# The prices of a list scheduler's calls, changed for three kinds of instruction, in a two-layer RWKV-7 trunk

## The chip, the cores and the metric

The kernel runs on one core of a Trainium2 chip. The metric is device time in microseconds: from the first to the last instruction of the program, plus what little lies around it. Three runs of the kernel before took 3034.83, 3038.67 and 3040.36 us, median 3038.67. One execution was profiled apart from these. Engines are named as in the profile: PE (TensorE matmuls), PEld (its weight loads), DVE (VectorE), ACT (ScalarE), POOL (GpSimd) and SP (SyncE, which only issues DMAs here).

## What is computed

One step of a hybrid decoder: a prompt of 16 + 512 rows and 8 sample rows go together through two layers of width 1024. All tensors are fp32. Each layer is

```
x = x + 0.5 * SwiGLU_1(RMSNorm(x))                          # d_ff 2816
x = x + W_o( sig(gA) * RWKV7(.) + sig(gB) * ShortConv(.) )  # the mixer
x = x + 0.5 * SwiGLU_2(RMSNorm(x))
```

with a last RMSNorm at the end. The recurrent part of the mixer, for 16 heads with a 64 x 64 state S each, is

```
Sa = S a_t
S  = S * w_t + Sa b_t^T + v_t k_t^T
y_t = S r_t
```

once from a zero state over the 528 prompt rows, and once for one step of 8 sample rows from given states.

## The kernel before

**Layout.** The 536 columns (528 prompt, 8 sample) lie along the free dimension, features along the 128 partitions. A fp32 product is made of three fp32r products: each operand is split into a high part (`hi`, a rounded copy by ACT) and a low part (`lo`, the rest, a subtraction on DVE), and `hi*hi + hi*lo + lo*hi` is summed. Weights arrive by DMA as `raw` and are split on the way.

**Stages.** The program alternates FFN stages (FFN 1 of layer 0; then the mixer; then FFN 2 of layer 0 and FFN 1 of layer 1; the mixer; FFN 2 of layer 1 and the last norm) with two mixer stages. An FFN stage is a stream of large fp32r matmuls.

**The mixer.** Heads are handled in eight pairs, p = 0 to 7. The 528 rows are cut into 11 chunks of 48. For each pair:

- `stage_k(p)`: projects k and r, forms decays, and by fp32 matmuls (`wg`) the triangular matrices of all chunks, `GT`. They go to DRAM (`td<-GT`) and come back in another layout (`Ta<-td`, `Tb<-td`). There the matrix I - T of all 22 chunk and head combinations is inverted by forward substitution on GpSimd: 47 steps of two dependent operations each, a product `pr<-Ta,Xinv` (later `pr<-Tb,Xinv`) and a sum `Xinv<-Xinv,pr`. There is one buffer each of `Ta`, `Tb` and `Xinv`. The inverse goes out by four DMAs `xd<-Xinv` and back by two, `Yd<-xd`; then `Xinv<-in_xid` loads the identity for the next pair.
- `stage_v(p)`: projects v and prepares per-chunk products (`wv`, `wg`, `wp`).
- `chain(p)`: the serial recurrence over the 11 chunks. Each chunk has five links through PE, all in tile `cq`: `cq<-mv,sd` (not in the first chunk), DVE `rh`, a transpose `cq<-cst,rh`, DVE `rd`, the product with the inverse `cq<-rd,Yd`, ACT `ud`, `cq<-GR,ud`, DVE `sx`, a transpose `cq<-cst,sx`, DVE `sd`. The last `sd` goes out as `out_o_swkv<-sd`.
- `gnorm(p)` normalises the chain's output (`wm` matmuls), `stage_m(p)` merges it with gates.

Beside these runs filler: 40 pieces of gates and short convolution (`gated_parts`, matmuls `acc<-xh,hi` and the like), handed out by a list per layer. After the last pair's projections `sample()` takes the 8 sample rows through one recurrent step: transposes, a trip through DRAM (`vd`, `VB`), then eight rounds of 512-column operations over the states `s`, mostly on GpSimd (`t` and `s` tiles; 88 such operations on GpSimd in the two layers together), another trip (`yd`, `yb`) and short norms. The tile `s` uses the buffer of `Ta`. The first half of the output projection w_o (`acc<-mh,hi` and the like, 192 matmuls) needs the sample's result and is the last filler of a mixer; the second half opens the next FFN stage.

**What sets the order.** Nothing is issued as it is written. Each call (`nc.vector.tensor_tensor(...)`) is put on a list by `Sched.add`, with a price from `Sched.price` (the time that the engine is thought to be busy) and its dependencies. At the end of a stage `flush` runs a list scheduling over five engines: it keeps a clock for each engine, takes the engine that is free first, and from the calls whose inputs and buffers are ready by its clock takes the one with the lowest priority number (`o.prio`: the place in the program less a `boost` for its kind of work). Time between engines is a table (`HOPS`). A result is ready for a dependent call on the same engine 0.1 to 0.15 us later. DMAs have a price on SP and a landing time. The order that comes out is fixed: each engine then executes its own queue in that order and waits at semaphores.

Prices of matmuls also go into `clocked`, which models PE's clock by the columns issued in steps of 3.4133 us. `self.ffn` is true within the body of an FFN; the change touches what is priced with it false, and the column count.

Of the kernel before, what the change touches and what calls it, by code (L numbers as in the profile page):

```python
# [8 lines left out]
F32R = mybir.dt.float32r  # L9
# [3 lines left out]
PSUM = bass.MemoryType.PSUM  # L13
# [83 lines left out]
class Sched:  # L97
# [41 lines left out]
    def price(self, eng, fn, out, ins, kw):  # L139
        n = self.width(out)  # L140
        if fn == "dma_start":
            return 0.48, 4 * n * out.shape[0] / self.DMA_RATE
        if eng == "tensor":
            if fn == "transpose" or kw.get("is_transpose"):
                return n / 1200 + 2e-3, self.HOP
            return (max(n, 256) / 2400 + (12e-3 if self.ffn else 2.3e-3) if ins[0].dtype == F32R else n / 600 + 6e-3), self.HOP
        if eng == "vector":
            if fn == "memset":
                return 8e-3 + n / 960, self.HOP
            if fn == "reciprocal":  # L150
                return 0.12 + n * 6.16e-3, self.HOP
            if fn == "tensor_reduce":
                n = self.width(ins[0])
            return (0.13 if len(ins) > 2 else 0.07) + n / 960, self.HOP
        if eng == "scalar":
            psum = any(x.tensor.space == PSUM for x in ins + [out])
            return (0.05 if psum else 0.095) + (0.09 if "scale" in kw else 0) + n / 1200, self.HOP
        if self.ffn:
            return 0.1 + n * 3.1e-3, self.HOP
        last = any(tuple(x.ap[-1])[0] == 0 for x in ins)  # L160
        return 0.155 + n * (1.63e-3 if last else 2.07e-3), self.HOP

    def add(self, eng, fn, args, kw):
        o = Op()
        o.seq, o.eng, o.fn, o.args, o.kw = len(self.ops), eng, fn, args, kw
        out = kw["out"] if "out" in kw else args[0]
        ins = [x for x in list(args) + list(kw.values()) if hasattr(x, "tensor") and x is not out]
        o.cost, o.lat = self.price(eng, fn, out, ins, kw)
        o.tab = TABLES.get(kw.get("func")) if eng == "scalar" else None
        o.succ, o.ready, o.prio, o.first, o.tiles, o.npred = [], 0.0, o.seq - self.boost, [], [], 0  # L170
        if eng == "tensor":
            o.cols0 = (o.cost - 2.3e-3) * 2400
            o.cols = o.cols0 * ins[0].shape[0] / 128
        w = (kw["lhsT"] if "lhsT" in kw else args[1]) if eng == "tensor" else None
        preds, needs, opens = {}, {}, {}
        for ap, wr in [(x, False) for x in ins] + [(out, True)]:
            t = ap.tensor
            if not hasattr(t, "tag_meta"):
                continue
            n = t.name  # L180
            if n not in self.acc:
                self.acc[n] = [], []
                if t.space != DRAM:
                    key = str(t.cap_key)
                    if key not in self.slots:
                        self.slots[key] = Slots(key.rsplit('_', 2)[1], t.bufs or t.tag_meta.bufs, self.gate)
                    self.life[n] = Life(self.slots[key], o)
                    self.slots[key].line.append(n)
                    o.first.append(n)
            if n not in o.tiles:  # L190
                o.tiles.append(n)
                if n in self.life:
                    lf = self.life[n]
                    lf.left += 1
                    opens[id(lf.opener)] = lf.opener
                    if n in lf.slots.held:
                        lf.slots.held[n] = None
            b = self.box(ap)
            writes, reads = self.acc[n]
            for c, q in writes + reads if wr else writes:  # L200
                if c[0] < b[1] and b[0] < c[1] and c[2] < b[3] and b[2] < c[3]:
                    preds[id(q)] = q
                    if not wr:
                        needs[id(q)] = 3 if ap is w and w.dtype == F32 else 2
            if wr:
                for a in (writes, reads):
                    a[:] = [x for x in a if not (b[0] <= x[0][0] and x[0][1] <= b[1] and b[2] <= x[0][2] and x[0][3] <= b[3])]
                writes.append((b, o))
            else:
                reads.append((b, o))  # L210

        for q in {**opens, **preds}.values():
            if q is o:
                continue
            kind = needs.get(id(q), 1 if id(q) in preds else 0)
            if q.succ is None:
                self.follow(q, o, kind)
            else:
                q.succ.append((o, kind))
                o.npred += 1  # L220
        self.ops.append(o)
# [1359 lines left out]
```

## Time and profile before

| | us |
|---|---|
| median of three runs | 3038.67 |
| profiled execution, its own time | 3028.59 |
| profiled execution, span | 3026.8 |
| mixer 1, from the end of the first FFN stage to the next | 395 to 1122 |
| mixer 2 | 1895 to 2626 |
| mean granted PE clock | 0.973 of full speed |

All five engines work side by side, so busy times overlap; matmul ends are modelled, so the starts of matmuls are the better measure. In the profile a fp32 matmul shows as two rows and a transpose as one. Buffer numbers are left out of names, so `mv0` and `mv1` are both `mv`. The views used: the head of the page, busy time by stretch of the span, waits by engine, groups by shape, and the timeline of one engine.

### The profile page before, as it was taken

To read this page: it belongs to the slowest core of one execution; us is meant where nothing else is said; L and a number is where in the kernel's file an instruction comes from. 1 tells how busy PE (TensorE), PEld (TensorE's weight loads), DVE (VectorE), ACT (ScalarE), POOL (GpSimd) and SP (SyncE) were. 2 spreads that over 40 slices of the span, in tenths; PEclk is the share of its full clock that TensorE was granted. 3 is DMA by queue.
4 is the path that set the end of the run, shared out by engine and by line. 5 is a ranking of instruction groups with operands and counts; after the bars stand their busy time and mean duration, and the time that the engine had idled before them with its cause. 6 is when DMAs were issued, how large, how long until landed. Compare 5 with 4: busy or idle time off the path is not lost. (4 is left out here: it accounts for less than half of the span.)

```text
span 3026.8 us, 56336 instructions
## 1 busy us (share of the span) xinstructions
PE 2835.8 (94%) x22146; PEld 2782.0 (92%) x22146; DVE 2170.7 (72%) x3995; ACT 1337.4 (44%) x2190; POOL 1043.2 (34%) x1886
## 2 busy tenths in 40 slices
PE   8999998988997899999999999999898988899997
PEld 8999998988897889999999999888888888899997
DVE  8777676766775868776687776766777659687774
ACT  5444453433443345444444444534444332554444
POOL 1000037776777811000100001477877778100001
PEclk9999999999999999999999999999999999999999
DMA  4233333223323462333323323332233133623232
GB/s 134 90 102 98 116 97 83 69 84 89 94 63 91 149 199 91 96 97 102 108 77 92 102 89 126 89 82 72 82 97 94 46 113 130 209 88 98 95 105 78
DMA packets 203802, 303.88 MB, mean 100 GB/s; under 512 B 102704, under 2 KB 110256, under 8 KB 203536
## 3 DMA queue, kind: packets, MB, share of 16 engines
q1 hardware_dynamic: 203536, 300.27, 32.7%
q8 instruction: 174, 2.85, 0.4%
q14 instruction: 92, 0.75, 0.1%
HBM read 264.49 MB, written 35.72 MB: 99 GB/s over the span
## 5 line engine op out<-in xcount | busy, mean ns | idle before, releaser
L268 ACT ACTIVATE hi<-raw 128x1024 fp32r<-128x1024 f32 (+4 forms) x460 | 387.4, 845 | 498.3 <-PE acc L268 188.9
L268 DVE TENSOR_TENSOR lo<-raw,hi 128x1024 fp32r<-128x1024 f32 (+4 forms) x460 | 461.0, 1004 | 78.6 <-ACT hi L268 71.8
L268 PE MATMUL acc<-xh,lo 128*128 128x268 f32 (+1 forms) x2112 | 484.5, 303 | 15.6 <-DVE lo L268 15.4
L268 PE MATMUL acc<-xh,hi 128*128 128x268 f32 (+1 forms) x2112 | 484.9, 304 | 11.4 <-ACT hi L268 4.8
L268 PE MATMUL acc<-xl,hi 128*128 128x268 f32 (+1 forms) x2112 | 482.3, 301 | 0.0
L268 POOL MEMSET wide<- 128x104 f32 (+1 forms) x7 | 1.3, 188 | 1328.7 <-DVE lo L268 1264.1
L268 POOL TENSOR_TENSOR Xinv<-Xinv,pr 88x140 f32<-88x140 f32 (+36 forms) x752 | 402.0, 535 | 54.8
L268 PEld LDWEIGHTS acc<-xh,lo 128*128 128x128 f32 x2112 | 350.2, 195 | 19.7 <-DVE lo L268 19.4
L268 PEld LDWEIGHTS acc<-xh,hi 128*128 128x128 f32 x2112 | 350.8, 195 | 16.8 <-ACT hi L268 8.3
L268 PEld LDWEIGHTS acc<-xl,hi 128*128 128x128 f32 x2112 | 348.4, 195 | 0.2
L268 PE MATMUL a<-hh,lo 128*128 128x268 f32 (+1 forms) x1408 | 287.6, 286 | 0.2 <-DVE lo L268 0.2
L268 PE MATMUL a<-hl,hi 128*128 128x268 f32 (+1 forms) x1408 | 287.2, 285 | 0.0
L268 PE MATMUL a<-hh,hi 128*128 128x268 f32 (+1 forms) x1408 | 286.5, 285 | 0.0
L268 POOL TENSOR_TENSOR pr<-Ta,Xinv 88x150 f32<-88x150 f32 (+21 forms) x384 | 200.0, 521 | 147.9 <-DMA Xinv<-in_xid 57.5
L268 PE MATMUL x<-xh,hi 128*128 128x268 f32 (+1 forms) x864 | 247.1, 286 | 1.6 <-ACT sn L268 1.6
L268 PE MATMUL x<-xl,hi 128*128 128x268 f32 (+1 forms) x864 | 247.0, 286 | 0.0
L268 PE MATMUL x<-xh,lo 128*128 128x268 f32 (+1 forms) x864 | 246.8, 286 | 0.0
L268 ACT ACTIVATE hi<-s 128x1024 fp32r<-128x1024 f32 x144 | 151.3, 1057 | 177.1 <-DVE s L268 101.3
L268 PEld LDWEIGHTS a<-hh,lo 128*128 128x128 f32 x1408 | 219.3, 188 | 0.5 <-DVE lo L268 0.4
L268 PEld LDWEIGHTS a<-hl,hi 128*128 128x128 f32 x1408 | 218.6, 188 | 0.0
L268 PEld LDWEIGHTS a<-hh,hi 128*128 128x128 f32 x1408 | 218.5, 188 | 0.0
L268 DVE TENSOR_TENSOR lo<-s,hi 128x1024 fp32r<-128x1024 f32 x144 | 173.4, 1221 | 16.5 <-ACT hi L268 15.7
(562 smaller groups left out, 7235.2 us busy)
## 6 DMA issues: line engine op xcount, KB each, us to landing
raw<-in_f_in SPq DMA_DIRECT2D x176, 512.0 KB
raw<-in_w_in SPq DMA_DIRECT2D x132, 512.0 KB
raw<-in_f_out SPq DMA_DIRECT2D x128, 256.0 KB
raw<-in_f_out SPq DMA_DIRECT2D x32, 384.0 KB
raw<-in_w_o SPq DMA_DIRECT2D x32, 256.0 KB
Ta<-td SPq DMA_DIRECT2D x64, 99.0 KB
XD<-X SPq DMA_DIRECT2D x16, 268.0 KB
s<-in_swkv SPq DMA_DIRECT2D x16, 256.0 KB
```

The source lines that it names most:

```text
L268: return getattr(getattr(self.nc, o.eng), o.fn)(*o.args, **o.kw)
```

## The change

Three prices change in `price`, and the count of columns in `add` follows.

```diff
         if eng == "tensor":
             if fn == "transpose" or kw.get("is_transpose"):
                 return n / 1200 + 2e-3, self.HOP
-            return (max(n, 256) / 2400 + (12e-3 if self.ffn else 2.3e-3) if ins[0].dtype == F32R else n / 600 + 6e-3), self.HOP
+            return (max(n, 256) / 2400 + 12e-3 if ins[0].dtype == F32R else n / 600 + 6e-3), self.HOP
...
-            return (0.13 if len(ins) > 2 else 0.07) + n / 960, self.HOP
+            fixed = 0.13 if len(ins) > 2 else 0.07
+            if not self.ffn and len(ins) > 1 and all(x.tensor.space != PSUM for x in ins):
+                return fixed + n / 860, self.HOP
+            return fixed + n / 960, self.HOP
...
         if self.ffn:
             return 0.1 + n * 3.1e-3, self.HOP
-        last = any(tuple(x.ap[-1])[0] == 0 for x in ins)
-        return 0.155 + n * (1.63e-3 if last else 2.07e-3), self.HOP
+        return 0.2 + n * 3e-3, self.HOP
...
-            o.cols0 = (o.cost - 2.3e-3) * 2400
+            o.cols0 = (o.cost - 12e-3) * 2400
```

Within the mixers a fp32r matmul of 268 columns is priced at 0.124 us instead of 0.114, a DVE operation of 528 columns with two SBUF inputs at 0.684 instead of 0.620, and a GpSimd operation of 140 columns at 0.62 instead of 0.44 (0.38 with a broadcast input), one of 512 columns at 1.74 instead of 1.21 (0.99). No call is added or removed; all engines' queues keep their instructions (ACT loses two of 77 table loads) and change their order in both mixers, while the FFN stages keep theirs but for a few rows.

Three places, all in mixer 1 (mixer 2 has the same pattern), are shown as the queue's rows in order: first before, then now.

GpSimd's queue near the end of the last pair's inversion. `pr` and `Xinv` are its steps; `s_6104`, `t_...`, with `VB`, are the sample's 512-column operations; `MBs`, `GSs` are small copies. Before:

```order
L268 TENSOR_TENSOR Xinv<-Xinv,pr 88x11x5
L268 TENSOR_TENSOR pr<-Tb,Xinv 88x44
L268 TENSOR_TENSOR Xinv<-Xinv,pr 88x11x4
L268 TENSOR_TENSOR pr<-Tb,Xinv 88x36
L268 TENSOR_TENSOR s_6104<-s_6104,VB 128x512
L268 TENSOR_TENSOR Xinv<-Xinv,pr 88x12x3
L268 TENSOR_TENSOR t_6106<-VB,sm_6093 128x512
L268 TENSOR_TENSOR pr<-Tb,Xinv 88x24
```

Now:

```order
L270 TENSOR_TENSOR Xinv<-Xinv,pr 88x11x5
L270 TENSOR_TENSOR t_6127<-VB 128x512
L270 TENSOR_TENSOR pr<-Tb,Xinv 88x44
L270 TENSOR_TENSOR Xinv<-Xinv,pr 88x11x4
L270 TENSOR_TENSOR t_6128<-s_6104,VB 128x512
L270 TENSOR_TENSOR pr<-Tb,Xinv 88x36
L270 TENSOR_TENSOR s_6104<-s_6104,VB 128x512
L270 TENSOR_TENSOR Xinv<-Xinv,pr 88x12x3
L270 TENSOR_TENSOR t_6130<-VB,sm_6093 128x512
L270 TENSOR_TENSOR pr<-Tb,Xinv 88x24
```

The sample's operations have moved in between the steps: 34 of them now stand inside this inversion, from its 54th operation on, where there were 4, from the 90th. In mixer 2 it is 42, from the 53rd, where there was none.

SyncE's queue at the end of pair 4's inversion. `out_o_swkv<-sd` stores the end state of a chain (before it is chain 3's, and now also chain 3's), `td<-GT` sends out a later pair's matrices (pair 6), `Yd_4735` takes pair 4's inverse. Before:

```order
L268 DMA Tb<-td 22x24x24
L268 DMA xd<-Xinv 264x1x48
L268 DMA Tb<-td 22x24x24 x3
L268 DMA raw<-in_w_in 128x1024
L268 DMA xd<-Xinv 264x1x48 x3
L268 DMA raw<-in_w_lora 128x128
L268 DMA Yd_4735<-xd 48x11x48 x2
L268 DMA Xinv<-in_xid 88x576
L268 DMA raw<-in_w_in 128x1024 x2
L268 DMA mbD<-z 128x528
L268 DMA mb<-mbD 128x528
L268 DMA out_o_swkv<-sd 128x128
```

Now:

```order
L270 DMA Tb<-td 22x24x24
L270 DMA xd<-Xinv 264x1x48
L270 DMA Tb<-td 22x24x24 x3
L270 DMA xd<-Xinv 264x1x48
L270 DMA out_o_swkv<-sd 128x128
L270 DMA xd<-Xinv 264x1x48 x2
L270 DMA td<-GT 48x11x48 x2
L270 DMA Yd_4735<-xd 48x11x48 x2
L270 DMA Xinv<-in_xid 88x576
```

The store of chain 3's end and the two `td` of pair 6 have moved from behind `Yd` and `Xinv` to ahead of them. The same pattern, with the pair before and the pair after next, stands at pairs 1 to 5 of both mixers; at pair 6 the store alone.

PE's queue at the start of the last pair's chain, chain 7. `Yd_4736` is its inverse and `Yd_4735` chain 6's; `acc<-xh,hi` and the like are projections, `wm` and `ws` small fp32 products of the norm and of the sample. Before:

```order
L268 MATMUL cq<-rd,Yd_4736 96x128
L268 MATMUL cq<-rd,Yd_4735 96x128
L268 MATMUL acc<-xh,lo 128x268 x2
L268 MATMUL acc<-xh,hi 128x268 x2
L268 MATMUL acc<-xl,hi 128x268
L268 MATMUL cq<-GR,ud 128x128 x2
L268 MATMUL acc<-xl,hi 128x268
L268 MATMUL acc<-xh,lo 128x268 x2
L268 MATMUL acc<-xh,hi 128x268 x2
L268 MATMUL cq<-cst,sx 128x128
L268 MATMUL acc<-xl,hi 128x268 x2
L268 MATMUL cq<-cst,sx 128x128
```

Now, from the end of `gnorm(6)` on, with chain 7's first two chunks:

```order
L270 MATMUL wm<-sl,cr 128x240
L270 MATMUL cq<-rd,Yd_4736 96x128
L270 MATMUL cq<-GR,ud 128x128
L270 MATMUL cq<-cst,sx 128x128
L270 MATMUL cq<-mv_4732,sd 128x160
L270 MATMUL ws<-cst,yb 128x8 x8
L270 MATMUL cq<-cst,rh 96x128
L270 MATMUL ws<-sm_6092,cr 128x64
L270 MATMUL cq<-rd,Yd_4736 96x128
L270 MATMUL ws<-sm_6092,cr 128x64
L270 MATMUL cq<-GR,ud 128x128
L270 MATMUL cq<-cst,sx 128x128
```

The projections have moved ahead of chain 7: 278 stood behind its first `Yd` matmul, and none does now (mixer 2: 262 and none). In their place the sample's transposes (`ws<-cst,yb`) stand between its first two chunks.

## The prediction

> **What bounds the kernel now.** The first view is the head of the page: busy time by engine, and the strip of 40 slices.
>
> ```profile
> span 3026.8 us, 56336 instructions
> PE 2835.8 (94%) x22146; PEld 2782.0 (92%) x22146; DVE 2170.7 (72%) x3995; ACT 1337.4 (44%) x2190; POOL 1043.2 (34%) x1886
> ...
> PE   8999998988997899999999999999898988899997
> ...
> POOL 1000037776777811000100001477877778100001
> ```
>
> TensorE is busy nearly throughout, but dips in two stretches, and GpSimd works in exactly those: the mixers. The busy time by stretch puts a feed-forward (FFN) window beside both mixers and one bad window.
>
> ```profile
> 200.00:250.00 50.00, 50.00 (x407) 49.99 (x407) 34.85 (x53) 22.16 (x36) 0.00 (x0) 1.00 0.31 96
> 395.00:1122.00 727.00, 647.97 (x4907) 628.31 (x4906) 518.90 (x1156) 298.86 (x535) 479.60 (x907) 0.96 0.34 99
> 1895.00:2626.00 731.00, 654.81 (x4919) 630.01 (x4918) 524.34 (x1143) 304.13 (x542) 493.71 (x922) 0.95 0.34 99
> 700.00:750.00 50.00, 38.06 (x276) 35.99 (x276) 30.78 (x74) 18.36 (x32) 29.84 (x66) 0.86 0.32 92
> ```
>
> Columns: stretch, length, then busy time (and instructions) of PE, PEld, DVE, ACT, POOL, then granted clock. In the FFN a fp32r matmul of 268 columns follows the last after 50/407 = 0.123 us, with no gap. In the mixers PE idles 79 and 76 us, and where it idles the clock falls too (0.86). So only the mixers can change: 1458 us of the span. Whom PE waits for in mixer 1 (us in total, times, longest):
>
> ```profile
> PE cq L268 <- ACT ud L268: 14.0, 5, 9.5
> PE cq L268 <- DVE P L268: 12.8, 9, 7.7
> ...
> PE wg L268 <- ACT P L268: 7.9, 1, 7.9
> ...
> PE wn L268 <- DVE kql L268: 6.1, 2, 5.5
> ```
>
> Four single waits (9.5, 7.7, 7.9, 5.5) make 30.6 of the 79 us. GpSimd, priced too low, stands behind the first: the timeline shows SyncE still from 697.57 until GpSimd's last read of `Tb` in an inversion, with the weights that ACT needs queued behind. For the other three I take the same cause, by VectorE's longest wait for GpSimd in this mixer.
>
> ```profile
> 697.57 0.32 SPq L268 DMA_DIRECT2D mb<-mbD  x1
> 710.32 0.32 SPq L268 DMA_DIRECT2D Tb<-td  x1
> ...
> 713.26 0.85 SPq L268 DMA_DIRECT2D raw<-in_w_in  x2
> ```
>
> ```profile
> 710.08 0.21 POOL L268 TENSOR_TENSOR pr<-Tb,Xinv 88x12 f32<-88x12 f32 x1
> ```
>
> ```profile
> DVE V L268 <- POOL sm L268: 8.6, 1, 8.6
> ```
>
> The second clock of a mixer is a ring: 94 dependent GpSimd operations invert one head pair's triangle, DMAs carry it out (`xd`) and into `Yd`, and the next `Xinv` is loaded into the one buffer. GpSimd's timeline, at the first and last inversion of each mixer:
>
> ```profile
> 443.77 0.26 POOL L268 TENSOR_TENSOR pr<-Ta,Xinv 88x47 f32<-88x47 f32 x1 [4.30 <-DMA raw<-in_w_in]
> ...
> 501.49 0.22 POOL L268 TENSOR_TENSOR Xinv<-Xinv,pr 88x12 f32<-88x12 f32 x1
> ...
> 514.52 0.26 POOL L268 TENSOR_TENSOR pr<-Ta,Xinv 88x47 f32<-88x47 f32 x1 [12.56 <-DMA Xinv<-in_xid]
> ...
> 938.83 0.26 POOL L268 TENSOR_TENSOR pr<-Ta,Xinv 88x47 f32<-88x47 f32 x1 [4.76 <-DMA raw<-in_w_in]
> ...
> 998.57 0.77 POOL L268 TENSOR_TENSOR Xinv<-Xinv,pr 88x12 f32<-88x12 f32 x1
> ...
> 1941.14 0.51 POOL L268 TENSOR_TENSOR pr<-Ta,Xinv 88x47 f32<-88x47 f32 x1 [3.22 <-DMA Ta<-td]
> ...
> 2436.17 0.26 POOL L268 TENSOR_TENSOR pr<-Ta,Xinv 88x47 f32<-88x47 f32 x1 [7.37 <-DMA Yd<-xd]
> ...
> 2490.06 0.21 POOL L268 TENSOR_TENSOR Xinv<-Xinv,pr 88x12 f32<-88x12 f32 x1
> ```
>
> Seven turns take 495.1 us in mixer 1 and 495.0 in mixer 2: **70.7 us a pair**. The last inversions end at 999.34 and 2490.27. PE's timeline shows when pair 0's chain first uses its inverse, and when the last pair's chain (chain 7) first uses its own and ends (x4: chains 6 and 7 together):
>
> ```profile
> 514.95 0.38 PE L268 MATMUL cq<-rd,Yd 96*96 96x128 f32 x2
> ...
> 1028.97 0.61 PE L268 MATMUL cq<-rd,Yd 96*96 96x128 f32 x4
> ...
> 1106.14 0.27 PE L268 MATMUL cq<-cst,sx 128*128 128x128 f32 x1
> ...
> 2531.24 0.60 PE L268 MATMUL cq<-rd,Yd 96*96 96x128 f32 x4
> ...
> 2604.32 0.27 PE L268 MATMUL cq<-cst,sx 128*128 128x128 f32 x1
> ```
>
> PE thus takes (1028.97 - 514.95)/7 = 73.4 us a pair, and lags behind the ring at the end. An inverse can be used 13.2 us after the inversion's end (pair 0: from 501.71 to 514.95). Chain 7 could have started at 1012.5 and 2503.5: it has **slack of 16.4 and 27.7 us**.
>
> **The change, term by term.** The new prices are nearer the trace (a 268-column matmul: 0.114 us before, 0.124 now, 0.123 in the trace). That they are true doesn't make the order good: the scheduler is greedy, and its priorities stay. No instruction is added; two table loads of ACT, which isn't the bound, go. The FFNs keep their order but for a few rows: nothing. What counts stands in the three places of the section on the change.
>
> *Term a, the last inversion.* Sample operations of 512 columns, one between two steps, now stand inside the last inversion: 34 in mixer 1, 42 in mixer 2, where before there were 4 and none. The next step waits behind each. Their groups:
>
> ```profile
> L268 POOL TENSOR_TENSOR t<-s,VB 128x512 f32<-128x512 f32 x24 | 38.4, 1603 | 16.7 <-DVE s L268 16.5 <-DMA VB<-vd 0.3
> ...
> L268 POOL TENSOR_TENSOR s<-s,t 128x512 f32<-128x512 f32 x16 | 25.9, 1618 | 0.2
> L268 POOL TENSOR_TENSOR s<-s,VB 128x512 f32<-128x512 f32 x16 | 23.4, 1464 | 1.9 <-DVE t L268 1.8
> L268 POOL TENSOR_TENSOR t<-VB 128x512 f32<-128x512 f32 x16 | 21.9, 1366 | 0.0
> ...
> L268 POOL TENSOR_TENSOR t<-VB,sm 128x512 f32<-128x512 f32 x16 | 20.5, 1278 | 0.0
> ```
>
> 88 operations take 130.1 us, 1.478 each: 30 x 1.478 = 44.3 and 42 x 1.478 = 62.1 us. Less the slack: 27.9 + 34.4 = **+62.3 us**.
>
> Part of the 1.478 is disturbance:
>
> ```profile
> L268 POOL TENSOR_TENSOR t<-s,VB x24: 1269/1307/3011, 999.3 to 2569.4; 128x512 f32<-128x512 f32 x24
> ```
>
> (minimum, median, maximum in ns). At minima, about 1.18 by estimate over the five groups, the term is 21 us less; I keep the means, since VectorE, though short of work there, still has the chain and the sample's reductions. The Trainium skill, "SBUF — State Buffer", section "SBUF: two separate sides", speaks against the size: a VectorE operation with two SBUF inputs and a GpSimd operation share a port pair by an exclusive lock, the loser blocks. By that rule a quiet VectorE gives the minima, and the sum below would be 54 instead of 75; the spread 1269 to 3011 fits it.
>
> *Term b, chain 7 itself.* Before, 278 and 262 projection matmuls stood between its links; now none does: they are all ahead, and only the 192 matmuls of w_o are left, which need the sample's result. 26 of its 53 links have under 0.5 us of other PE work, before 1 and 2. Bare, a chain runs at its own latency, shown by its ACT step at the start and the end of the fastest two chunks in a row:
>
> ```profile
> 2592.33 0.27 ACT L268 ACTIVATE ud<-cq 96x128 f32<-96x128 f32 x1 [0.82 <-PE cq L268]
> ...
> 2602.61 0.27 ACT L268 ACTIVATE ud<-cq 96x128 f32<-96x128 f32 x1 [2.08 <-PE cq L268]
> ```
>
> That is 10.28/2 = 5.14 us a chunk: 10 x 5.14 + 3.4 for the last links = 54.8 us, against 77.2 and 73.1 before: -22.4 and -18.3. Two things lengthen it, 5 us each as estimates: its matmuls run at half clock where PE is idle (about 0.93 us a chunk doubled over five bare chunks; the row of 700 to 750 shows such a clock), and the `yb` transposes, which need the sample's end (six of its operations follow the inversion, 8.9 us, and two DMAs), now stand in front of the second chunk. Term b: -40.7 + 20 = **-20.7 us**; without the two, -40.7.
>
> *Term c, the ring's pace.* Before, SyncE issues `Yd` and the next `Xinv` ahead of `out_o_swkv` (the end of the previous chain) and of `td` (a later pair's k stage). Now both stand ahead of `Yd`: the ring waits for PE at every turn, and PE for the ring. PE needs per pair 73.4 us, plus 207 more matmuls in seven pairs (278 projections less 71 of w_o: 25.4/7 = 3.6 us), plus 23 more bare links in chains 0 to 6 at about 0.9 us each (3.0 us): 80 us if every old stall stays. If the four GpSimd stalls go (4.4 us a pair) and the half-clock ticks behind them (2.4, estimate), it is 73.2. Ends: 80 and the ring's 70.7 or, with nothing blocked, less: the shortest inversion
>
> ```profile
> 2368.32 0.26 POOL L268 TENSOR_TENSOR pr<-Ta,Xinv 88x47 f32<-88x47 f32 x1 [2.81 <-issue]
> ...
> 2420.24 0.21 POOL L268 TENSOR_TENSOR Xinv<-Xinv,pr 88x12 f32<-88x12 f32 x1
> ```
>
> took 52.1 us, with the 12.56 gap 64.7. I take 73.1, near before's own 73.4, since these stalls were GpSimd's: 2.4 x 14 turns = **+34 us**.
>
> Sum: 62.3 - 20.7 + 34 = **+75 us**. The profiled execution took 3028.59 us; the median of three runs lies 10.1 higher. Counted on it: 3038.67 + 75 = **3114 us**.
>
> **Rivals.**
> - *Faster, because true prices take the stalls away.* For: the 30.6 us of mixer 1 named above. Place: the ring's turn. Without term c the sum is +41.6, so it decides at 70.7 - 41.6/14 = 67.7 us a pair. At 66.5 it gives 41.6 - 58.8 = -17: 3022 us. Against: `out_o_swkv` and `td` ahead of `Yd` can only add waits to the ring. Chance 0.12.
> - *The work only changes place.* The instructions are the same; if the sample in POOL's second half of the inversion waits so little that term a falls to its minima (41), and the pace stays at 70.7 without half-clock losses, 41 - 41 + 0 = 0: about 3038, within 0.2% (what a measurement of this kernel can tell from no change). Chance 0.05.
> - *Both couplings in full.* PE's stalls stay and each turn takes 80: 9.3 x 14 = 130, sum +172: 3211 us. For: 28 bare links in chains 0 to 6 of mixer 1 against 5. Chance 0.12.
> - The forecast, slower by 20 to 150: 0.71.
>
> **Numbers.** Predicted 3114 us. The forecast's own range is 3045 to 3190: below, minima in term a and a pace of 70.7 (75 - 21 - 34 = +20, so 3059) and most of the 20 us that lengthen chain 7; above, a pace of 78.5 (41.6 + 109). That leaves out 0.29, so the range given reaches down past the faster rival, to 3015; full coupling stays outside. Faster 0.12, within 0.2% 0.05, slower 0.83.
>
> **What would show it.** Term a: in the changed profile the last inversions take about 104 and 116 us (before 60.5 and 54.1), with `t` and `s` operations between steps, and PE waits for DMA `Yd` or for `yb` in one long stretch before chain 7. Term b: chain 7 lasts about 65 us at a low clock. Term c: starts of inversions 73 us apart, and SyncE waiting for DVE `sd` ahead of `Yd`. Wrong, if inversions start under 68 us apart, or if PE has other work during the last inversion.

## The result, and the profile after

The changed kernel takes 3155.56 us (median of 4 runs, 3148.86 to 3156.45) against 3037.99 for the kernel before on the same chip: a ratio of 1.0383, 95% interval 1.0365 to 1.0401, or +117.6 us. The forecast was 3114, with 3015 to 3190 as its range. The profiled execution took 3148.86.

The head of its page: busy time by engine, then the strip of 40 slices, with the granted clock.

```profile
span 3147.1 us, 56358 instructions
PE 2876.4 (91%) x22146; PEld 2796.5 (89%) x22146; DVE 2181.5 (69%) x3995; ACT 1334.2 (42%) x2188; POOL 1029.9 (33%) x1886
...
PE   8999998999999279999999999999899991799998
...
POOL 1000146777776701000100001576667667000001
PEclk9999999999999679999999999999899995799998
```

Each mixer now ends in a hole (a 2 and a 1 in PE's row) with the clock down to 0.5 or 0.6. Where the time goes is seen by cutting a mixer at three points: the first step of pair 0's inversion, the first step of pair 7's (seven turns of the ring lie between), chain 7's first use of its inverse, and the start of w_o's second half. Busy time in these stretches, before (mixer 1, then 2):

```profile
443.80:938.80 495.00, 441.09 (x3351) 430.10 (x3350) 344.29 (x805) 201.33 (x361) 355.95 (x734) 0.95 0.30 84
938.80:1028.97 90.17, 75.71 (x573) 71.95 (x571) 66.46 (x134) 24.37 (x46) 80.78 (x125) 0.96 0.34 106
1028.97:1116.00 87.03, 80.01 (x603) 76.66 (x602) 65.75 (x143) 40.85 (x83) 31.50 (x28) 0.96 0.56 178
1941.10:2436.20 495.10, 444.23 (x3301) 428.57 (x3300) 345.73 (x795) 213.06 (x372) 364.00 (x742) 0.94 0.30 83
2436.20:2531.24 95.04, 82.45 (x619) 78.87 (x618) 70.03 (x141) 25.00 (x48) 83.18 (x131) 0.93 0.35 110
2531.24:2616.20 84.96, 75.77 (x587) 71.01 (x586) 67.59 (x139) 37.73 (x82) 36.82 (x31) 1.00 0.53 175
```

The same stretches in the changed kernel:

```profile
444.40:974.40 530.00, 499.77 (x3769) 480.48 (x3768) 377.21 (x856) 224.59 (x396) 374.22 (x743) 0.97 0.32 89
974.40:1103.60 129.20, 66.01 (x466) 61.06 (x465) 78.88 (x138) 22.26 (x44) 95.48 (x144) 0.75 0.32 97
1103.60:1171.60 68.00, 53.45 (x297) 43.98 (x298) 31.48 (x92) 18.14 (x50) 0.00 (x0) 0.73 0.33 113
1995.50:2539.90 544.40, 505.35 (x3737) 483.15 (x3736) 378.28 (x855) 233.31 (x406) 367.72 (x750) 0.95 0.31 87
2539.90:2670.40 130.50, 62.81 (x484) 59.39 (x483) 78.59 (x130) 23.84 (x44) 102.61 (x151) 0.76 0.26 81
2670.40:2737.50 67.10, 51.64 (x298) 42.00 (x299) 31.36 (x92) 19.31 (x51) 0.19 (x1) 0.73 0.42 140
```

Columns: stretch, length, then busy time (and rows) of PE, PEld, DVE, ACT and POOL, then the granted clock. The six stretches grew by 121.9 us together, which is the whole difference of the spans (120.3). Read by length: turns +35.0 and +49.3, last inversion up to chain 7's first product +39.0 and +35.5, chain 7 and what is left -19.0 and -17.9.

Read by PE: in the turns PE does 418 and 436 rows more than before and is busy 94% and 93% of the time instead of 89% and 90%. These rows are missing at the end: from the last inversion's start on PE has 763 and 782 rows where it had 1176 and 1206. PE's idle time (length less busy) falls by 23.7 and 11.8 us in the turns, and rises by 56.3 and 61.4 behind them: +82.1 in all. The other 39.8 us are PE busy for longer with nearly the same rows (9,051 against 9,034). At the end, where the clock is 0.73 to 0.76 instead of 0.93 to 1.00, a row takes longer: the chain's last transpose 0.47 us (the row at 1163.55 below) where it took 0.27. How much of the 39.8 is the clock, and how much is rows that no longer overlap, was not separated.

GpSimd's timeline, first and last inversions, answers to that of before:

```profile
444.42 0.26 POOL L270 TENSOR_TENSOR pr<-Ta,Xinv 88x47 f32<-88x47 f32 x1 [1.98 <-DMA Ta<-td]
...
974.40 0.26 POOL L270 TENSOR_TENSOR pr<-Ta,Xinv 88x47 f32<-88x47 f32 x1 [3.82 <-DMA Xinv<-in_xid]
...
1092.33 0.55 POOL L270 TENSOR_TENSOR Xinv<-Xinv,pr 88x12 f32<-88x12 f32 x1
...
1995.51 0.73 POOL L270 TENSOR_TENSOR pr<-Ta,Xinv 88x47 f32<-88x47 f32 x1 [0.54 <-DMA Ta<-td]
...
2539.93 0.31 POOL L270 TENSOR_TENSOR pr<-Ta,Xinv 88x47 f32<-88x47 f32 x1 [1.75 <-DMA Xinv<-in_xid]
...
2659.45 0.66 POOL L270 TENSOR_TENSOR Xinv<-Xinv,pr 88x12 f32<-88x12 f32 x1
```

Turns are 530.0/7 = **75.7** and 544.4/7 = **77.8 us** (before 70.7), the last inversions **118.5** and **120.2 us** long (before 60.5 and 54.1). PE's timeline at chain 7's first product with its inverse and at its end:

```profile
1103.57 0.71 PE L270 MATMUL cq<-rd,Yd 96*96 96x128 f32 x2 [47.59 <-DMA Yd<-xd]
...
1163.55 0.47 PE L270 MATMUL cq<-cst,sx 128*128 128x128 f32 x1 [0.50 <-DVE P L270]
...
2670.42 0.71 PE L270 MATMUL cq<-rd,Yd 96*96 96x128 f32 x2 [51.11 <-DMA Yd<-xd]
...
2729.40 0.47 PE L270 MATMUL cq<-cst,sx 128*128 128x128 f32 x1 [0.50 <-DVE P L270]
```

PE stands still for 47.59 and 51.11 us until the last inverse lands: the two largest waits of the kernel. The chain then takes 60.0 and 59.0 us.

Inside the last inversion GpSimd's timeline shows two delays, not one:

```profile
1028.12 1.67 POOL L270 TENSOR_TENSOR t<-s,VB 128x512 f32<-128x512 f32 x1 [7.13 <-DVE s L270]
1029.75 0.44 POOL L270 TENSOR_TENSOR pr<-Tb,Xinv 88x144 f32<-88x144 f32 x1
1030.15 1.30 POOL L270 TENSOR_TENSOR s<-s,VB 128x512 f32<-128x512 f32 x1
1031.41 0.47 POOL L270 TENSOR_TENSOR Xinv<-Xinv,pr 88x144 f32<-88x144 f32 x1
1031.84 1.04 POOL L270 TENSOR_TENSOR t<-VB,sm 128x512 f32<-128x512 f32 x1
...
1044.53 1.29 POOL L270 TENSOR_TENSOR t<-s,VB 128x512 f32<-128x512 f32 x1 [6.48 <-DVE s L270]
```

Each step waits for the sample's operation ahead of it; and three times in this mixer the whole queue waits 6 to 7 us (7.13, 6.48 and 5.99) for VectorE's sum `s`, which in turn needs GpSimd's `t`. The five groups of 512-column operations:

```profile
L270 POOL TENSOR_TENSOR t<-s,VB 128x512 f32<-128x512 f32 x24 | 32.8, 1366 | 37.6 <-DVE s L270 35.7 <-PE cq L270 1.9
L270 POOL TENSOR_TENSOR s<-s,VB 128x512 f32<-128x512 f32 x16 | 20.3, 1269 | 0.0
L270 POOL TENSOR_TENSOR s<-s,t 128x512 f32<-128x512 f32 x16 | 20.2, 1263 | 0.0
L270 POOL TENSOR_TENSOR t<-VB,sm 128x512 f32<-128x512 f32 x16 | 17.0, 1063 | 3.0 <-PE cq L270 2.0 <-DVE sm L270 1.1
L270 POOL TENSOR_TENSOR t<-VB 128x512 f32<-128x512 f32 x16 | 16.6, 1038 | 0.0
```

106.9 us for 88 operations: 1.215 us each (before 1.478); the wait for `s` is 35.7 us (before 16.5). The sample's operations got shorter, and their waits longer.

### The profile page after: what moved, and what is told of

It reads as the page before. It is cut to its first block, busy times and chain, and to the rows that moved or that the text cites. A ratio compares the mean times of both kernels' runs of the same rounds, so it can differ in the third digit from the quotient of the medians.

```text
span 3147.1 us, 56358 instructions
## 1 busy us (share of the span) xinstructions
PE 2876.4 (91%) x22146; PEld 2796.5 (89%) x22146; DVE 2181.5 (69%) x3995; ACT 1334.2 (42%) x2188; POOL 1029.9 (33%) x1886
## 4 chain that ended last, share of the span: by engine, by line
PE 71%; DVE 12%; POOL 5%; DMA 4%; ACT 4%; issue 3%; SPq 1%; DVEq 0%; ACTq 0%; POOLq 0%
PE acc L270 21%; PE a L270 15%; PE x L270 11%; PE y L270 5%; PE cq L270 5%; DVE lo L270 3%; PE au L270 3%; DMA raw<-in_f_in 3%; PE z L270 3%; PE ag L270 3%; PE wg L270 3%; PE wp L270 1%; POOL Xinv L270 1%; POOL pr L270 1%; DVE s L270 1%
## 5 line engine op out<-in xcount | busy, mean ns | idle before, releaser
L270 PE MATMUL acc<-xh,hi 128*128 128x268 f32 (+1 forms) x2112 | 475.6, 301 | 21.3 <-ACT hi L270 4.2
L270 DVE TENSOR_TENSOR lo<-raw,hi 128x1024 fp32r<-128x1024 f32 (+4 forms) x460 | 454.7, 990 | 54.5 <-ACT hi L270 48.1
L270 PE MATMUL acc<-xh,lo 128*128 128x268 f32 (+1 forms) x2112 | 476.6, 300 | 7.3 <-DVE lo L270 7.2
L270 PE MATMUL acc<-xl,hi 128*128 128x268 f32 (+1 forms) x2112 | 472.7, 299 | 0.0
L270 POOL TENSOR_TENSOR Xinv<-Xinv,pr 88x140 f32<-88x140 f32 (+36 forms) x752 | 388.6, 517 | 50.6
L270 PEld LDWEIGHTS acc<-xh,hi 128*128 128x128 f32 x2112 | 343.6, 193 | 30.8 <-ACT hi L270 9.4
L270 PEld LDWEIGHTS acc<-xh,lo 128*128 128x128 f32 x2112 | 343.9, 192 | 11.8 <-DVE lo L270 11.7
L270 ACT ACTIVATE ud<-cq 96x128 f32<-96x128 f32 x176 | 47.4, 269 | 388.8 <-PE cq L270 388.6
```

What stands on the lines that cost most here:

```text
L270: return getattr(getattr(self.nc, o.eng), o.fn)(*o.args, **o.kw)
```

## The experiments

Ratios are against the kernel before on the same chip. The kernel before had medians of 3036.96, 3032.74 and 3039.57 us in the three sets of four. "Turns" and "last inversions" are read from each run's GpSimd timeline, as above.

### First set: which price, and which place

**GpSimd's price alone.** The kernel before with only

```diff
-        last = any(tuple(x.ap[-1])[0] == 0 for x in ins)
-        return 0.155 + n * (1.63e-3 if last else 2.07e-3), self.HOP
+        return 0.2 + n * 3e-3, self.HOP
```

> The kernel before with GpSimd's new price alone; the matmul and VectorE prices stay. In its order 34 and 42 sample operations of 512 columns stand inside the last inversions (before 4 and 0; changed kernel 34 and 42), no projection matmul stands behind chain 7's first Yd, and out_o_swkv or td stand ahead of Yd at 11 of 14 turns. Theory 'GpSimd's price does it all': as slow as the changed kernel, 3120 to 3180 us, last inversions 115 to 122 us long, turns of the ring 75 to 78 us. Rival 'the three prices share the cost': between, 3060 to 3110 us. Rival 'matmul price': 3040 us.

Measured 3189.61 us, ratio 1.0502 (1.0485 to 1.0520). Turns 78.5 and 80.3 us, last inversions 113.6 and 121.4. This price alone costs 153 us, more than the whole change and above the theory's range: the pattern was expected, not that the other prices would take some of it back.

**The matmul and VectorE prices alone.** The change without that edit.

> The matmul price (with its column count) and VectorE's price as changed, GpSimd's price as before. In its order no sample operation stands inside an inversion and SyncE's queue has out_o_swkv behind Yd at every turn, as before; 363 and 408 projection matmuls stand behind chain 7's first Yd, and none of w_o's first half (before 121 and 102). Theory 'GpSimd's price does it all': within 1% of before, 3010 to 3070 us, turns 69 to 72 us, last inversions 53 to 61 us. Rival 'the three prices share the cost': 3070 to 3110 us.

Measured 3080.89, ratio 1.0141 (1.0123 to 1.0159): above the main theory's range and inside the rival's, though turns (72.2 and 71.7 us) and last inversions (54.9 and 55.0 us) are nearly those of before. The time lies behind chain 7: from its end to w_o's second half it takes 28.8 and 35.6 us, before 9.9 and 11.9, since the last projections now run until 1119.6 and 2639.1, and w_o's first half comes only then. That is 42.6 us of a difference of 43.9 (46.2 between the profiled spans), and a cost that the forecast didn't have.

**The last inversion unbroken.** The changed kernel; a flag on the inversion's calls makes the next step count as ready at once. The same edit with `p < KD - 1` gives the run after this one.

```diff
+            if q.tie and o.tie:
+                d = 0.0
             if kind == 3 and q.eng != "tensor":
...
+                nc.tie = p == KD - 1
                 for st in range(C - 1):
```

> The changed kernel, in which the scheduler counts the next step of the last pair's inversion as ready at once (0 instead of 0.1 us), so that nothing comes between its steps; the sample's operations follow it. Turns 1 to 6 as in the changed kernel, chain 7 nearly bare (52 and 49 bare links of 53) and out_o_swkv of chain 6 ahead of its Yd. Theory (term a): the last inversions fall from 119 to about 58 us, chain 7 starts about 50 us earlier, but the sample ends only some 65 us after the inversion and w_o's first half (192 matmuls, 24 us) follows it, so about 33 us a mixer come back: 3090 us (3070 to 3110). Rival 'the ring's pace alone costs the time, PE needs the sample anyway': 3140 to 3160 us. Rival 'all of term a comes back': 3030 us.

Measured 3124.10, ratio 1.0283 (1.0268 to 1.0299): +87 instead of +118, so 30 us come back, not 66: between the ranges of the theory and of its rival. Its stretches in mixer 1, cut as above:

```profile
448.70:976.10 527.40, 496.65 (x3755) 477.26 (x3753) 375.92 (x854) 225.09 (x396) 379.77 (x742) 0.97 0.32 89
976.10:1041.20 65.10, 61.48 (x462) 58.70 (x461) 38.83 (x96) 17.42 (x33) 47.09 (x103) 0.95 0.32 97
1041.20:1159.40 118.20, 67.51 (x304) 48.13 (x303) 65.76 (x138) 26.10 (x67) 51.14 (x41) 0.61 0.34 111
```

The inversion is down to 52.2 us, and from its start to chain 7's first product it takes 65.1 us instead of 129.2. But the third stretch grows by 50: the sample's last operation moves from 1099.8 to 1120.7, and w_o's first half runs from 1134.3 to 1159.3 with nothing else on PE (304 rows in 118 us). Whichever of the two goes first on GpSimd, PE waits for the other, because the work that used to lie beside both has already run.

**Inversions 0 to 6 unbroken.**

> The changed kernel, with the steps of the inversions of pairs 0 to 6 kept together in the same way, the last one not. No small copy stands within those seven inversions (5 to 14 before); SyncE has out_o_swkv ahead of Yd at one turn only, td at none; 16 and 7 sample operations stand in the last inversion; 109 and 280 projections behind chain 7's first Yd. Theory (term c is made by the copies within the inversion and by the two transfers ahead of Yd): turns fall from 75.7 and 77.8 to 68 to 71 us, the time to 3010 to 3060 us. Rival 'the ring is slow because PE has more work in it': turns stay at 74 to 78, the time stays above 3110 us.

Measured 3198.08, ratio 1.0527 (1.0503 to 1.0551). Both theories fail: the turns became longer, 79.7 and 80.7 us, with each inversion at only 49 to 55. GpSimd's waits in mixer 1's turns say why (us in total, times, longest):

```profile
POOL NS L273 <- DVE ps__5193 L273: 19.9, 1, 19.9
POOL MBs L273 <- DVE z L273: 17.4, 3, 9.3
POOL NS L273 <- DVE ps__5700 L273: 16.4, 1, 16.4
```

The small copies now stand between two inversions instead of inside them, and there the next inversion waits behind them, up to 20 us at a time, for what VectorE makes of later projections. Nor is PE full: in these turns it has 3303 and 3195 rows (before 3351 and 3301) and is busy only 82% and 81% of the time. An order without copies inside the inversions is not an order without waits.

### Second set: what in GpSimd's price, and what in the turns

**Only the inversion's price new.** The kernel before, with the new formula for the 94 steps of each inversion and the old one for all other GpSimd operations.

> The kernel before with the new GpSimd price for the 94 steps of each inversion alone (33.2 to 49.1 us a pair in the price list); every other price as before, the sample's too. In its order 34 and 42 sample operations stand inside the last inversions and out_o_swkv or td ahead of Yd at 11 of 14 turns. Theory 'the inversion's price carries it all': as with GpSimd's whole price, 3160 to 3200 us. Rival 'the sample's price and the small copies carry a good part': below 3120 us.

Measured 3177.57, ratio 1.0477 (1.0459 to 1.0495). Turns 79.0 and 80.5 us, last inversions 111.7 and 112.2. The inversion's price carries nearly all of GpSimd's 153 us.

**Only the inversion's price old.** The changed kernel with the old formula for these steps.

> The changed kernel with the old GpSimd price for the steps of the inversions alone; all other prices as changed. No sample operation inside an inversion, no out_o_swkv or td ahead of Yd; 347 and 302 projection matmuls behind chain 7's first Yd, none of w_o's first half. Theory 'the inversion's price carries it all': near the run with the matmul and VectorE prices alone (3081 us), 3060 to 3095, turns 68 to 72 us. Rival 'the other prices on GpSimd cost too': above 3110 us.

Measured 3064.16, ratio 1.0097 (1.0077 to 1.0116). Turns 72.3 and 70.9 us, last inversions 52.3 and 53.0. It costs 31 us instead of 118: one price in the table decides 86 of them.

**The old inversion price times 1.1.**

> The kernel before with the old price of the inversion's steps times 1.1 (33.2 to 36.5 us a pair), all else as before. 25 and 39 sample operations stand inside the last inversions and 28 and 0 projections behind chain 7's first Yd, nearly as in the changed kernel; but SyncE's queue has neither out_o_swkv nor td ahead of Yd at any turn, as before. Theory A, the two transfers ahead of Yd make the turns long: turns stay at 70 to 72 us, only terms a and b are paid, 3065 to 3095 us. Theory B, the work that is pulled into the turns makes them long (PE is full in them): turns of 74 to 78 us, 3120 to 3160 us.

Measured 3091.37, ratio 1.0193 (1.0175 to 1.0211): theory A's time. The last inversions take 98.1 and 113.3 us, and the turns 72.3 and 73.7, above A's 70 to 72. Its turns, both mixers:

```profile
446.10:952.50 506.40, 459.60 (x3435) 446.04 (x3434) 352.70 (x820) 203.44 (x363) 360.74 (x734) 0.95 0.30 85
...
1966.80:2482.70 515.90, 463.22 (x3539) 450.65 (x3538) 359.51 (x832) 219.50 (x385) 371.18 (x745) 0.96 0.31 86
```

PE has 84 and 238 rows more in the turns than before (changed kernel: 418 and 436), and the turns are 11.4 and 20.8 us longer (35.0 and 49.3). So this run does not separate queue from work as it was meant to: it has no transfer ahead of `Yd`, but it also pulls less work into the turns than the count behind chain 7 suggested.

**The matmul price alone.**

> The kernel before with the matmul price (and its column count) alone changed. No sample operation inside an inversion, no transfer ahead of Yd but td at one turn; 341 and 426 projections behind chain 7's first Yd and none of w_o's 192 (before 121 and 102 of them there). Theory 'w_o pushed behind chain 7 is what the matmul and VectorE prices cost together (44 us)': 3065 to 3090 us here. Rival 'VectorE's price is what costs': 3030 to 3045 us.

Measured 3072.16, ratio 1.0125 (1.0105 to 1.0145). From chain 7's end to w_o's second half 38.5 and 29.5 us: the cost of the second run, in its place.

### Third set: what makes the turns long

**The stores on ScalarE's queue.** The changed kernel with

```diff
-                    S.dma_start(out=td[h].rearrange("c s t -> s c t"), in_=GT[h * C:(h + 1) * C, :, :])
+                    A.dma_start(out=td[h].rearrange("c s t -> s c t"), in_=GT[h * C:(h + 1) * C, :, :])
...
-                S.dma_start(out=io["o_swkv"][l, p], in_=sd)
+                A.dma_start(out=io["o_swkv"][l, p], in_=sd)
```

> The changed kernel, with out_o_swkv and the two td of each pair issued from ScalarE's queue instead of SyncE's; the order keeps 34 and 43 sample operations in the last inversions and no projection behind chain 7's first Yd, but nothing stands on SyncE between xd and Yd for PE's sake any more. In the changed kernel Yd was issued 9.0 to 13.5 us after an inversion's end, before mostly 7 to 9. Theory 'the transfers ahead of Yd make the turns longer than in the run with 1.1 times the inversion's price (72.3 and 73.7)': turns fall from 75.7 and 77.8 by 2 to 4 us, 3100 to 3130 us. Rival 'PE is full in the turns, the queue doesn't matter': turns stay, 3145 to 3165 us.

Measured 3154.70, ratio 1.0379 (1.0357 to 1.0400): nothing changes. The edit did what it should: `Yd` is issued 8.9 us after an inversion's end, mean of 14 turns (changed 10.7, before 9.1), and ScalarE stood still for these stores only twice, 8.4 us in all, in mixer 1. But the turns are 76.2 and 77.2 us:

```profile
446.10:979.80 533.70, 500.88 (x3790) 480.67 (x3790) 382.27 (x861) 228.47 (x400) 376.05 (x742) 0.97 0.32 90
2002.80:2543.10 540.30, 504.34 (x3769) 483.79 (x3768) 379.42 (x856) 230.09 (x404) 377.45 (x750) 0.96 0.32 88
```

PE's rows and busy time in them are those of the changed kernel. What the hand-over (from an inversion's end to the next one's start) saved, the inversions gave back: those of pairs 0 to 6 grew from 60.5 to 62.5 us (mixer 1) and from 62.4 to 63.9. In mixer 1 GpSimd's waits inside them, counting those over 0.7 us, account for most of it (24.9 us instead of 13.4, mainly of copies that wait for VectorE); in mixer 2 these waits hardly moved (33.0, 32.3), and why those inversions grew is open.

**The small copies on ScalarE.** The changed kernel with each `G.tensor_copy` of `NS`, `SGA`, `pe`, `CVP`, `CVS`, `MBs` and `GSs` written as `A.activation(..., func=AF.Copy)`.

> The changed kernel, with the small copies (NS, SGA, pe, CVP, CVS, MBs, GSs: 2 to 11 columns) done by ScalarE instead of GpSimd; 0 to 4 other operations are left within an inversion of pairs 0 to 6, SyncE's order as in the changed kernel. In the changed kernel waits of such copies for VectorE, ScalarE or PE stopped the inversions for 13.5 and 32.4 us a mixer (before 2.1 and 0.8). Theory 'these waits lengthen the turns': turns fall by 2 to 4.5 us, 3105 to 3130 us. Rival 'PE is full in the turns': turns stay, 3145 to 3165 us.

Measured 3137.40, ratio 1.0318 (1.0301 to 1.0335): +98 instead of +118, so 20 us come back. Turns 74.3 and 76.6 us, 1.5 and 1.2 less; the inversions of mixer 1 shrink from 60.5 to 57.9 us, and the hand-overs grow from 15.2 to 16.3. Less than the theory said, more than the rival. The edit did not take the waits away, though: those over 0.7 us inside the inversions fell only from 13.4 to 8.0 us (mixer 1) and from 32.3 to 26.4, since other GpSimd operations, `z<-z,cs` and `ka<-k,a`, now wait there for ScalarE and PE.

**VectorE's price alone.**

> The kernel before with VectorE's price alone changed; 240 and 289 projections and 113 and 126 of w_o's matmuls behind chain 7's first Yd (before 278, 262 and 121, 102), no sample operation inside an inversion. If costs add up: 44 less the 39 of the matmul price, so 3030 to 3050 us. Rival 'any other order than the one that the boosts go with costs some 1%': 3060 to 3080 us.

Measured 3053.10, ratio 1.0041 (1.0027 to 1.0056): +13.5, just above the sum's range. Alone the three prices cost 153, 39 and 13.5 us, 206 in all; together 118. They don't add up.

**The old inversion price times 0.9.**

> The kernel before with 0.9 times the old price of the inversion's steps; 291 and 411 projections, 121 and 4 of w_o's matmuls behind chain 7's first Yd, nothing inside an inversion. Theory 'a price below the true one gives the ring slack, and more slack is better': 3000 to 3030 us. Rival 'the lists and boosts fit the old price, and a step either way costs': 3045 to 3080 us.

Measured 3092.76, ratio 1.0174 (1.0159 to 1.0190). The rival's answer, and beyond its range: a lower price is no safer than a higher one. With 0.9, 1.0 and 1.1 times the old price the time is +53, 0 and +59 us. Much of the +53 lies in the turns: they take 72.8 and 74.5 us, though PE has fewer rows in them than before (3261 and 3177, before 3351 and 3301) and is busy only 86% and 85% of the time; the hand-overs are 16.5 and 17.2 us long, before 13.8 and 14.2. No run was faster than the kernel before.

## Why the prediction was right, and where it was off

The sign, the place and the mechanism of terms a and b were right; all three terms had the forecast's sign. The size was not: the sum is some 45 us short of the spans' difference, and that it is not further off is partly luck, since a and c came out 68 us dearer and b and the hand-over 23 us cheaper. By the same steps, with the rows above (forecast, measured; the sum is the difference of the two profiled spans, and the line above it is what the three terms leave):

| step | forecast | measured |
|---|---|---|
| a: longer last inversions less slack | +62.3 | +80.0 (+58.0 + 66.1 - 44.1) |
| b: chain 7 | -20.7 | -31.3 (-17.2 - 14.1) |
| c: seven turns, two mixers | +34 | +84.3 (+34.9 + 49.4) |
| hand-over of the last inverse, end and start of the mixers | 0 | -12.7 |
| sum | +75 | +120.3 |

- **What bounds the kernel.** Only the mixers changed: the six stretches hold all of the difference. Right.
- **Term a.** Forecast lengths 104 and 116 us, measured 118.5 and 120.2. One size was too large and one missing. The 34 and 42 operations take 41.5 and 50.7 us, 1.21 us each instead of 1.478. The wait for VectorE's `s` inside the inversion (19.6 us in mixer 1, 15.3 in mixer 2) was not counted. The Trainium skill, "SBUF — State Buffer", section "SBUF: two separate sides", calls the port pair that VectorE and GpSimd share an exclusive lock. The trace fits this, for the size that was too large: from the sample's first 512-column operation to its last VectorE is busy 58% of the time in both mixers (50.69 of 87.80 us and 53.10 of 92.20), before 88% and 94% (68.19 of 77.70 and 76.13 of 80.80), and the medians of the five groups, 1.04 to 1.29 us, are now near their former minima, 1.03 to 1.28. No run changed VectorE's load alone.
- **PE during the last inversion.** One of the forecast's signs of being wrong, other work on PE there, half came: PE still has 341 and 359 projection rows in the stretches that begin with it and is busy for 66.01 and 62.81 us. Only behind them comes the long wait that terms a and b described.
- **Term b.** The bare pace was right (59 to 60 us, with 54.8 as the floor); what lengthens it, counted as 20 us in all, was 9.4. The row cited for a half clock (700 to 750) shows 0.86 on average, not a half; the stretches that hold chain 7 now show 0.73.
- **Term c is the step that was wrong**, in size and in part of its reason. The forecast held that `out_o_swkv` and `td` ahead of `Yd` make the ring wait at every turn. The run with these stores on another queue undoes that and gains nothing. The other half of the reason, that PE has more to do in the turns, stands, and was mis-sized: 207 more matmuls in seven turns were counted, from what stood behind chain 7's first `Yd`, less 71 of w_o. By the order, matched to the trace, the turns hold 355 and 360 more matmuls of 256 columns and up. The 71 should not have been taken off (w_o's 192 lie behind the turns in both kernels), and 58 and 75 more came from the stretch of the last inversion. 150 more at 0.123 us over seven turns are 2.6 us a turn: 73.1 becomes 75.7, mixer 1's measured turn. Mixer 2's 77.8 has 2 us more. This is arithmetic after the fact, on top of 73.1, which rested on estimates; no run moved the projections alone.
- **What holds the turns at 76 us** is not fully settled. Taking the transfers away gave 0, the small copies 20 us (with other waits in their place), and each time part of the gain reappeared in the other half of the ring, while PE stayed 93 to 95% busy. Both at once was not tried, and whether the turn is then PE's work alone stays open. Added work is not the only thing that makes a turn long: with 0.9 times the price, and with inversions 0 to 6 unbroken, turns were longer than in the kernel before, with fewer rows on PE and more idle time.
- **Rivals.** "Faster, because true prices take the stalls away": the four single waits are gone from PE's list, and PE's idle time in the turns fell by 35.5 us; but the ring did not speed up, and the end lost more. "The work only changes place" is the nearest in words: work moved from the end into the turns; it costs 118 us, and not nothing, because of what it left behind. Full coupling at 80 us a turn was too pessimistic for the changed kernel, though GpSimd's price alone gave 78.5 and 80.3.
- **The matmul price** was costed at nothing of its own. Alone it costs 39 us, with w_o's first half pushed behind chain 7; in the changed kernel w_o runs within chain 7 (1114.6 to 1145.7), so this cost does not show in its 118 us.

Was the new price false? For the inversion it is nearly true: by the formulas the 94 steps come to 33.2 us at the old price and 49.1 at the new, or 42.5 and 58.4 with the 0.1 us between steps; the inversions of the kernel before took 56.8 on average. For the sample's operations it is too high (1.74 us against 1.04 to 1.37). The runs show that the truer number for the inversion alone makes the order worse by 145 us. That a longer inversion makes the scheduler see PE free during the turns, so that it fills them with projections, fits the 355 and 360 matmuls that moved; the scheduler's own clocks were not read out, so this link is argued.

## What to carry to other kernels

A truer price is not a better order: a greedy list scheduler fills the gap that it sees first, so what matters is which work is left for the last wait, where nothing else can cover it. Look there first, for the longest single wait and for what had covered it. Boosts and lists go with the prices at which they were chosen: here 10% more or less on one price cost 1.7 to 1.9%, which suggests changing prices and boosts together (not tried here). And before a queue's order is blamed for a slow ring, count the work that was moved into the ring and the idle time of the engine that is thought full: removing one of several waits may only hand the time to the next.

## What was not expected

- Small copies that wait for another engine stop GpSimd's dependent chain: 13.4 and 26.7 us of waits over 0.7 us each inside the inversions of pairs 0 to 6 (before 2.1 and 0.8; a larger operation, `ka<-k,a`, adds 5.6 in mixer 2), and up to 19.9 us at once when they were moved between the inversions.
- A 512-column GpSimd operation took 1.478 us on average beside a busier VectorE and 1.215 in the changed kernel, the same operations on the same data.
- PE's granted clock fell to 0.61 over a whole stretch of 118 us in which it had 304 rows and was busy for 67.51 us.
